# Tall Strassen sets: third sum formed in place, first sum asked for earlier, p5 ahead of q6, gate reads in program order

## The chip, the cores and the metric

The kernel runs on one core of one Trainium2 chip. A core has five engines that run their own instruction streams and meet at semaphores: PE (TensorE, matrix products), DVE (VectorE), ACT (ScalarE), POOL (GpSimd) and SP (SyncE), the last of which only issues DMA transfers here. The profile shows PE's weight loads apart as PEld. The metric is the device time of one execution in microseconds (us).

## The reference

One block of a hybrid network on 512 tokens of width 1024, all in float32. Cut to what matters here:

```python
x = x + 0.5 * swiglu(rmsnorm(x, g1), ffn1_w_gu, ffn1_w_down)
h = rmsnorm(x, g_mix)
z = h @ w_in                                  # 1024 x IN_COLS
cb, cc, cu, q, k, v, g_lr, r, ga, gb = split(z)
y_conv = (cb * causal_short_conv(cc * cu, conv_w)) @ w_out_conv
log_a = log_sigmoid(g_lr @ gate_w_up + gate_b) / 16
o = gla_chunked(q, k, v, log_a)               # 4 heads, chunks of 64 tokens
o = norm_per_head(o) * gla_norm_g
y_gla = (o * silu(r)) @ w_out_gla
merged = sigmoid(ga) * y_conv + sigmoid(gb) * y_gla
x = x + merged @ w_o
x = x + 0.5 * swiglu(rmsnorm(x, g2), ffn2_w_gu, ffn2_w_down)
return rmsnorm(x, g_final)
```

The change lies in the middle part: the products for v, ga, gb (columns of `w_in`, each 1024 x 1024) and `w_out_conv`, called out here.

## The kernel before

**Products.** Every float32 product is made of three matmuls on parts of the operands: a high part (a cast) and a low part (the operand less its high part). For a block of weights ACT makes the high part `wh` (L380) and DVE the low part `wl` (L381); three buffers of each are there. PE multiplies high x high, high x low and low x high.

**Sets of seven.** Most products are made in sets: the weights are cut in four blocks a11, a12, a21, a22 (512 KB each), and seven products of sums of blocks, m1 p2 q6 p5 q7 p3 p4, take the place of eight. A set needs these weight operands:

- m1: a11; then POOL asks for a transfer that accumulates in SBUF, a11 += a21 (`add`, L355; a21 holds a21 + a22 by then)
- p2: a12; then a12 += a11
- q6: a11 as it is by then; p5: a21, which is a21 + a22; p4: a22; p3: a12 as it is by then
- q7: s3 = a11 + a21 of the first values, made by DVE into a fifth tile (L365)

So a set has three accumulating transfers on POOL's queue: a21 += a22 (asked right after L365), a11 += a21 (after m1's low part), a12 += a11 (after p2's low part and a11's sum).

**Tall sets.** v, ga, gb and out are "tall": each has two halves, s = 0 and 1, with weights of their own, and their products alternate (`tall`): m1 of half 0, m1 of half 1, p2 of half 0, and so on, 14 steps of 12 matmuls of 128x512 on PE (L691). The other sets (conv, cb, r; PE line L575) have one half and 24 matmuls of 128x256 a step. In time the order is: v, ga, gb, then conv 0 to 3, cb, r, and out, and then the set for `w_out_gla`.

**What sets the order.** `Weights(2)` issues, while PE is at one step, the weight work of the step two places ahead: loads on SP's queue (L351) into tiles named f (ten in the pool), sums, cast and low part. Each engine takes its instructions in order, so a waiting instruction holds all behind it. A dictionary of hooks hangs pieces of the attention behind named steps: `gates`, `decays`, `scale`, `scores`, `state`, `output`, `squares` for each of four heads. `state` multiplies on PE (L1249) and copies from PSUM on DVE (L1252); `scale` and `decays` are chains on DVE (L546, L1190, L1193) and ACT. Results ga and gb are written to DRAM and read back by `gate()` on SP's queue (L1522), with a sigmoid on ACT behind it. A scheduler may move instructions against this order where data allow it; `keep_in_program_order` forbids it for one instruction.

**Loads of a tall set.** Half 0 is loaded four steps ahead of its m1 and half 1 three, and at m1 itself (issue step i) L365 and a21 += a22 are issued.

Of the kernel before, what the change touches and what calls it, by code (L numbers as in the profile page):

```python
# [12 lines left out]
ALU = mybir.AluOpType  # L13
# [56 lines left out]
def unit_cols(u):  # L70
    return u[2] * len(u[3]) * u[4]
# [57 lines left out]

TALL_ORDER = ("m1", "p2", "q6", "p5", "q7", "p3", "p4")
TALL = {}


# [81 lines left out]
def block_kernel(ctx: ExitStack, tc: tile.TileContext, xT, vecs, gf, gup, wgl, wts, out):  # L217
    nc = tc.nc
# [78 lines left out]
    class Weights:  # L297
# [3 lines left out]
        def __init__(self, ahead):  # L301
            self.ahead = ahead
            self.issued = 0
            self.taken = 0
            self.end = 0
            self.ready = []
            self.raw = {}
            self.loads = {}
            self.sums = {}
            self.pre = {}  # L310

        def phase(self, early, first=6):


            self.early = early
            lo, self.end = self.end, [e for e in ENDS if e > self.end][0]
            for i in range(lo, self.end):
                n, p = STEPS[i]
                if p == "m1" and i in CHUNK_STEP.values():
                    at = CHUNK_STEP[0, "m1"]  # L320
                    self.loads.setdefault(at - (4 if i == at else 2), []).append(n)
                    self.sums.setdefault(i, []).append(n)
                elif p == "m1" and n in TALL:
                    self.loads.setdefault(i - (4, 3)[TALL[n][1]], []).append(n)
                    self.sums.setdefault(i, []).append(n)
                elif p is None and i > lo and STEPS[i - 1][1] is not None and self.end < len(STEPS):
                    self.pre.setdefault(i - 4, []).append(n)
                elif p == "m1":
                    self.loads.setdefault(max(lo, i - first), []).append(n)
                    first = 6  # L330
                    self.sums.setdefault(max(lo + 3, i - 3), []).append(n)
            if self.end == len(STEPS):
                c = CHUNK_STEP
                for i, at in enumerate((c[1, "q6"], c[1, "p3"], c[1, "p3"], c[1, "p4"])):
                    self.pre.setdefault(at, []).append(STEPS[self.end - TAIL + i][0])
            self.fetch(lo)
# [20 lines left out]
        def issue(self):  # L357
            at = self.issued
            self.fetch(at)
            for n in self.loads.get(at, ()):  # L360
                self.raw[n] = [self.dma(n + i) for i in range(4)]
            for n in self.sums.get(at, ()):
                self.raw[n].append(tile_of("f", [P, 1024]))
                a11, a12, a21, a22, s3 = self.raw[n]
                nc.vector.tensor_tensor(out=s3, in0=a11, in1=a21, op=ALU.add)  # L365
                self.add(a21, a22)
            for n in self.pre.get(at, ()):
                self.raw[n] = self.dma(n)
            n, p = STEPS[at]
            w = unit_cols(PLAN[n])  # L370
            if p is None:
                raw = self.raw[n]
            else:
                a11, a12, a21, a22, s3 = (self.raw[n] + [None])[:5]
                raw = {"m1": a11, "p2": a12, "q6": a11, "p5": a21, "q7": s3, "p4": a22,
                       "p3": a12}[p]
            late = at >= len(STEPS) - TAIL
            h = tile_of("op" if late else "wh", [P, 1024], F32R)
            l = tile_of("op" if late else "wl", [P, 1024], F32R)
            nc.scalar.copy(h[:, :w], raw[:, :w])  # L380
            nc.vector.tensor_tensor(out=l[:, :w], in0=raw[:, :w], in1=h[:, :w].bitcast(F32),  # L381
                                    op=ALU.subtract)
            if p == "m1":
                self.add(a11, a21)
            if p == "p2":
                self.add(a12, a11)
            self.issued += 1
            self.ready.append((h, l))
# [657 lines left out]
    def mixer(norm, nxt):  # L1046
# [3 lines left out]
        gates_d = {n: dram.tile([KD, P, S], F32, tag=n, name=n) for n in ("ga", "gb")}  # L1050
# [19 lines left out]
        def G_tile(i, dtype=F32):  # L1070
# [13 lines left out]
            out=maskf, in_=maskf, pattern=[[1, P]], compare_op=ALU.is_ge, fill=0.0,  # L1084
# [13 lines left out]
        for i in range(2):  # L1098
# [3 lines left out]
                                    in1=gl_w[i][:, :, 0, :RANK].bitcast(F32), op=ALU.subtract)  # L1102
# [3 lines left out]
        for i in range(6):  # L1106
# [3 lines left out]
                                in1=gup_w[R2 : 2 * R2].bitcast(F32), op=ALU.subtract)  # L1110
# [18 lines left out]
        def evac_k(h, o):  # L1129
# [7 lines left out]
                                in1=glr[2 * R2 : R3].bitcast(F32), op=ALU.subtract)  # L1137
# [35 lines left out]
        def gates(h):  # L1173

            a = AUX()
            nc.tensor.matmul(a, gup_w[:R3, h * DK : (h + 1) * DK], glr[:R3],
                             start=True, stop=True)
            b = vec[:, V_GB + h : V_GB + h + 1]
            nc.scalar.activation(E, a, AF.Abs, bias=b)
            nc.vector.tensor_scalar(out=M, in0=a, scalar1=b, scalar2=0.0,  # L1180
                                    op0=ALU.add, op1=ALU.min)
            nc.scalar.activation(E, E, AF.Exp, scale=-1.0)
            nc.scalar.activation(E, E, AF.Ln, bias=1.0)
            nc.vector.tensor_tensor(out=M, in0=M, in1=E, op=ALU.subtract)
            nc.vector.tensor_tensor_scan(out=E, data0=reset, data1=M, initial=0.0,
                                         op0=ALU.mult, op1=ALU.add)
# [18 lines left out]
        def scale(h):  # L1205

            q_, k_ = QK[h][:, 0], QK[h][:, 1]
            ref, dc = sm4[:, 0], sm4[:, 1]  # L1210
            mul(q_, EX, q_)
            mul(KX, pairs(KS)[:, :, 0], pairs(k_)[:, :, 0])
            mul(QX, pairs(q_)[:, :, 1], bc(ref[:, :, 1]))
            mul(pairs(KS)[:, :, 1], pairs(KS)[:, :, 1], pairs(k_)[:, :, 1])
            mul(k_, M, k_)
            mul(pairs(KS)[:, :, 0], KX, bc(dc[:, :, 1]))
            mul(pairs(QS)[:, :, 1], QX, bc(dc[:, :, 0]))
            mul(pairs(QS)[:, :, 0], pairs(q_)[:, :, 0], bc(ref[:, :, 0]))
            mul(d2s, dc[:, :, 0], dc[:, :, 1])
# [59 lines left out]
        def squares(h):  # L1279

            sh, sl = split(E)
            st = AUX()
            nc.tensor.matmul(st, ones_r, sh, start=True, stop=False)
            nc.tensor.matmul(st, ones_r, sl, start=False, stop=True)
            nc.vector.transpose(E, st)
            nc.vector.tensor_scalar(
                out=vs[:, 16 * h : 16 * (h + 1)],
                in0=E.rearrange("p (b c) -> p b c", c=32)[:, :, 0],
                scalar1=1.0 / DV, scalar2=EPS, op0=ALU.mult, op1=ALU.add)
# [81 lines left out]
        def split_o(h):  # L1371
            for a, b in split_pair(O[h]):
                og_h.append(a)
                og_l.append(b)

        hooks = {
            ("v", 0, "q6"): [decays], ("v", 1, "p5"): [lambda: scale(0)],
            ("v", 1, "p3"): [lambda: scores(0)],
            ("ga", 1, "m1"): [lambda: state(0)], ("ga", 1, "p2"): [lambda: output(0)],
            ("ga", 0, "p5"): [lambda: squares(0)], ("ga", 0, "q7"): [lambda: gates(1)],  # L1380
            ("ga", 1, "q7"): [decays], ("ga", 1, "p3"): [lambda: scale(1)],
            ("gb", 0, "m1"): [lambda: scores(1)], ("gb", 0, "p2"): [lambda: state(1)],
            ("gb", 1, "q6"): [lambda: output(1)], ("gb", 1, "q7"): [lambda: squares(1)],
            ("gb", 0, "p3"): [move], ("gb", 0, "p4"): [lambda: gates(2)],
            ("gb", 1, "p4"): [decays], (0, "q6"): [lambda: scale(2)],
            (0, "p3"): [lambda: scores(2)], (1, "q6"): [lambda: state(2)],
            (1, "q7"): [lambda: output(2)], (1, "p3"): [lambda: squares(2)],
            (2, "q6"): [lambda: gates(3)], (2, "q7"): [decays], (2, "p3"): [lambda: scale(3)],
# [1 line left out]
            (4, "q6"): [lambda: output(3)], (4, "p3"): [lambda: squares(3)],  # L1390
            (5, "q7"): [lambda: normalise(0)], (5, "p3"): [lambda: normalise(1)],
            (6, "q7"): [lambda: normalise(2)], (6, "p3"): [lambda: normalise(3)],
            ("out", 1, "q6"): [lambda: co.make("p4")], ("out", 1, "p5"): [lambda: split_o(0)],
            ("out", 1, "q7"): [lambda: split_o(1)], ("out", 0, "p3"): [lambda: split_o(2)],
            ("out", 1, "p3"): [lambda: split_o(3)],
        }
# [117 lines left out]
        co = Operands(lambda j, l: YS[:, 4 * j : 4 * j + 4, 2 + l * HW : 2 + (l + 1) * HW])  # L1514
# [4 lines left out]

        def gate(name, t, e):  # L1520
            g = T()
            nc.sync.dma_start(g, gates_d[name][2 * t + e])  # L1522
            nc.scalar.activation(g, g, AF.Sigmoid)
            return g

# [31 lines left out]
        for e in range(2):  # L1557
            o = mm_wide("w_out_gla", KD, 512 * e, og_h, og_l, extra=between(e))
            for t in range(NTB):
                g = gate("gb", t, e)  # L1560
# [82 lines left out]
```

## Time and profile before

| | us |
|---|---|
| median of 3 runs | 1191.41 |
| lowest, highest | 1190.86, 1192.36 |
| the profiled execution | 1191.23 |
| its span in the trace | 1189.5 |

The profile is of one execution. Its page gives each engine's busy time; the view of waits says for how long PE stood idle and which instruction ended that; the timelines list instructions with start, duration and the idle time before them in brackets; the windows view gives the busy time of every engine in a stretch. Names such as `wl<-f,wh` are the program's own: output, then inputs, without buffer numbers. Lines L... are those of the kernel before.

The stages of interest, by PE: v from about 370 to 428 us, ga to 477, gb to 521, conv 0 from there, out from about 690 to 735.

### The profile page before, as it was taken

How to read it: one execution, taken by the hardware profiler on the slowest of the kernel's cores; microseconds unless marked ns; L12 is line 12 of the kernel's file. 1: busy time of each engine (PE TensorE's matmuls, PEld its weight loads, DVE VectorE, ACT ScalarE, POOL GpSimd, SP SyncE). 2: the span in 40 equal slices, each digit the busy share in tenths (PEclk: the TensorE clock that was granted, in tenths of full speed). 3: DMA queues.
4: the chain of work that ended last, by engine and by line, in shares of the span. 5: the costliest groups of instructions: out<-in, count | busy, mean ns of one | idle time of the engine just before them, and what ended most of it. 6: DMA issues, size and time to landing. Idle time of an engine off the chain costs nothing. (4 is left out here: it accounts for less than half of the span.)

```text
span 1189.5 us, 18127 instructions
## 1 busy us (share of the span) xinstructions
PE 1173.1 (99%) x7218; PEld 1052.5 (88%) x7218; DVE 917.9 (77%) x1132; ACT 619.3 (52%) x780; POOL 116.6 (10%) x155
## 2 busy tenths in 40 slices
PE   9999999999999999999999999999999999999997
PEld 8899999999988888789999997888889999998886
DVE  7987676989797976667787998556598767785686
ACT  6565455545452847464654568324356555572353
POOL 0011111011110110111010110100001111100100
PEclk9999999999999999999999999999999999999999
DMA  9378777656481885877567768712538777763431
GB/s 347 79 212 183 190 180 193 172 128 164 96 301 60 187 179 170 220 187 195 134 163 164 179 170 242 257 46 93 182 82 210 171 181 178 188 172 115 92 93 71
DMA packets 58148, 197.03 MB, mean 166 GB/s; under 512 B 6768, under 2 KB 6896, under 8 KB 58064
## 3 DMA queue, kind: packets, MB, share of 16 engines
q1 hardware_dynamic: 36912, 124.27, 31.0%
q0 software_dynamic: 18560, 67.12, 30.6%
q10 hardware_dynamic: 2592, 4.49, 1.0%
q8 instruction: 56, 0.92, 0.3%
q14 instruction: 28, 0.23, 0.1%
HBM read 124.55 MB, written 8.39 MB: 112 GB/s over the span
## 5 line engine op out<-in xcount | busy, mean ns | idle before, releaser
L380 ACT CAST wh<-f 128x1024 fp32r<-128x1024 f32 (+1 forms) x337 | 352.0, 1047 | 418.4 <-PE mm L575 93.2
L381 DVE TENSOR_TENSOR wl<-f,wh 128x1024 fp32r<-128x1024 f32 (+1 forms) x337 | 409.3, 1217 | 167.2 <-ACT wh L380 159.0
L575 PE MATMUL mm<-op,wh 128*128 128x256 f32 x1344 | 243.7, 284 | 0.8 <-ACT tp L580 0.8
L575 PEld LDWEIGHTS mm<-op,wh 128*128 128x128 f32 x1344 | 210.0, 192 | 1.5 <-ACT tp L580 1.0
L605 PE MATMUL mm<-op,wh 128*128 128x256 f32 x1152 | 209.7, 284 | 0.2 <-ACT tp L609 0.2
L355 POOL DMA_DIRECT2D f<-f x120 | 103.6, 869 | 947.4 <-DVE wl L381 457.7
L575 PE MATMUL mm<-op,wl 128*128 128x256 f32 x672 | 190.6, 284 | 1.4 <-DVE wl L381 1.4
L605 PEld LDWEIGHTS mm<-op,wh 128*128 128x128 f32 x1152 | 179.2, 191 | 2.1 <-ACT tp L609 0.6
L605 PE MATMUL mm<-op,wl 128*128 128x256 f32 x576 | 163.0, 283 | 0.1
L597 PE MATMUL mm<-op,wh 128*128 128x512 f32 x432 | 154.4, 398 | 0.0
L691 PE MATMUL mm<-wh,op 128*128 128x512 f32 x448 | 141.3, 391 | 0.8 <-ACT wh L380 0.8
L575 PEld LDWEIGHTS mm<-op,wl 128*128 128x128 f32 x672 | 128.9, 192 | 1.9 <-DVE wl L381 1.8
L599 PE MATMUL mm<-op,wl 128*128 128x256 f32 x432 | 121.4, 281 | 0.0
L605 PEld LDWEIGHTS mm<-op,wl 128*128 128x128 f32 x576 | 110.2, 191 | 0.3 <-DVE wl L381 0.3
L691 PEld LDWEIGHTS mm<-wh,op 128*128 128x128 f32 x448 | 84.1, 188 | 18.6 <-ACT wh L380 1.4
L597 PEld LDWEIGHTS mm<-op,wh 128*128 128x128 f32 x432 | 81.3, 188 | 18.2
L691 PE MATMUL mm<-wl,op 128*128 128x512 f32 x224 | 88.1, 393 | 1.7 <-DVE wl L381 1.7
L599 PEld LDWEIGHTS mm<-op,wl 128*128 128x128 f32 x432 | 81.7, 189 | 0.0
L432 PE MATMUL mm<-op,wh 128*128 128x512 f32 x256 | 64.3, 392 | 0.0
L408 PE MATMUL mm<-op,wh 128*128 128x512 f32 x164 | 63.8, 389 | 0.0
L409 PE MATMUL mm<-op,wh 128*128 128x512 f32 x164 | 63.8, 389 | 0.0
L410 PE MATMUL mm<-op,wl 128*128 128x512 f32 x164 | 63.8, 389 | 0.0
(288 smaller groups left out, 1641.8 us busy)
## 6 DMA issues: line engine op xcount, KB each, us to landing
f<-wts SPq DMA_DIRECT2D x219, 512.0 KB, 4.4
f<-f POOLq DMA_DIRECT2D x120, 512.0 KB, 5.0
X<-xT SPq DMA_DIRECT2D x8, 256.0 KB, 5.5
xs<-X POOLq DMA_DIRECT2D x8, 256.0 KB, 4.5
ga<-tp ACTq DMA_DIRECT2D x8, 256.0 KB, 2.4
gb<-tp ACTq DMA_DIRECT2D x8, 256.0 KB, 5.2
tp<-ga SPq DMA_DIRECT2D x8, 256.0 KB, 3.4
tp<-gb SPq DMA_DIRECT2D x8, 256.0 KB, 3.9
```

The lines of the kernel that those rows point to most:

```text
L355: nc.gpsimd.dma_start(out_, a, accum_op=ALU.add)
L380: nc.scalar.copy(h[:, :w], raw[:, :w])
L381: nc.vector.tensor_tensor(out=l[:, :w], in0=raw[:, :w], in1=h[:, :w].bitcast(F32), op=ALU.subtract)
L408: nc.tensor.matmul(o, wh, ah, start=first, stop=False)
L409: nc.tensor.matmul(o, wh, al, start=False, stop=False)
L410: nc.tensor.matmul(o, wl, ah, start=False, stop=last)
L432: nc.tensor.matmul(o[c], w[:, s : s + P], a[k], start=k == 0 and j == 0, stop=k == kt - 1 and j == 2)
L575: nc.tensor.matmul(to, ww[:, s], aa[:, t], start=fresh and k == 0 and e == 0 and j == 0, stop=k == 3 and j == 2, skip_group_check=True)
L597: nc.tensor.matmul(o[:, e], h[:, s], a, start=fresh and k == 0, stop=False, skip_group_check=True)
L599: nc.tensor.matmul(o[:, e, HW:], l[:, s], a[:, :HW], start=False, stop=k == 3, skip_group_check=True)
L605: nc.tensor.matmul(to, ww[:, s], aa, start=fresh and k == 0 and e == 0 and j == 0, stop=k == 3 and j == 2, skip_group_check=True)
L691: nc.tensor.matmul(self.bank[b][e], aa[:, c], ww, start=fresh and i == 0 and n == 0, stop=k == 3 and n == 2, skip_group_check=True)
```

## The change

1. In tall sets the fifth tile and L365 are gone. q7's operand is made in place from the sum in a11: a11 = (a11 + a21 + a22) − a22, by a DVE subtraction (line 381 of the new file), issued when q7's cast is. It follows the last readers of that sum: q6's cast and low part, and the transfer a12 += a11.
2. The first sum, a21 += a22, is asked for one issue step ahead of m1 in half 0 and in m1's own step in half 1 (two and three steps behind the loads), without waiting for a DVE instruction.
3. The order of the seven products in tall sets becomes m1 p2 p5 q6 q7 p3 p4.
4. Hooks of the fourth to seventh step are renamed to the products that now stand there; three move besides: gates(2) from behind (gb, 0, p4) to behind (gb, 1, p3), its `decays` from (gb, 1, p4) to (gb, 0, p4), and split_o(0) from (out, 1, p5) to (out, 0, q7).
5. The gate reads are kept in program order.

```diff
-TALL_ORDER = ("m1", "p2", "q6", "p5", "q7", "p3", "p4")
+TALL_ORDER = ("m1", "p2", "p5", "q6", "q7", "p3", "p4")
...
                 elif p == "m1" and n in TALL:
                     self.loads.setdefault(i - (4, 3)[TALL[n][1]], []).append(n)
-                    self.sums.setdefault(i, []).append(n)
+                    self.firsts.setdefault(i - (1, 0)[TALL[n][1]], []).append(n)
...
+            for n in self.firsts.get(at, ()):
+                self.add(self.raw[n][2], self.raw[n][3])
...
                 a11, a12, a21, a22, s3 = (self.raw[n] + [None])[:5]
+                if n in TALL:
+                    s3 = a11
+                    if p == "q7":
+                        nc.vector.tensor_tensor(out=a11, in0=a11, in1=a22, op=ALU.subtract)
...
-            ("v", 0, "q6"): [decays], ("v", 1, "p5"): [lambda: scale(0)],
+            ("v", 0, "p5"): [decays], ("v", 1, "q6"): [lambda: scale(0)],
...
-            ("ga", 0, "p5"): [lambda: squares(0)], ("ga", 0, "q7"): [lambda: gates(1)],
+            ("ga", 0, "q6"): [lambda: squares(0)], ("ga", 0, "q7"): [lambda: gates(1)],
...
-            ("gb", 1, "q6"): [lambda: output(1)], ("gb", 1, "q7"): [lambda: squares(1)],
-            ("gb", 0, "p3"): [move], ("gb", 0, "p4"): [lambda: gates(2)],
-            ("gb", 1, "p4"): [decays], (0, "q6"): [lambda: scale(2)],
+            ("gb", 1, "p5"): [lambda: output(1)], ("gb", 1, "q7"): [lambda: squares(1)],
+            ("gb", 0, "p3"): [move], ("gb", 1, "p3"): [lambda: gates(2)],
+            ("gb", 0, "p4"): [decays], (0, "q6"): [lambda: scale(2)],
...
-            ("out", 1, "q6"): [lambda: co.make("p4")], ("out", 1, "p5"): [lambda: split_o(0)],
+            ("out", 1, "q6"): [lambda: co.make("p4")], ("out", 0, "q7"): [lambda: split_o(0)],
...
             g = T()
-            nc.sync.dma_start(g, gates_d[name][2 * t + e])
+            tc.keep_in_program_order(nc.sync.dma_start(g, gates_d[name][2 * t + e]))
```

What this does to the order on the engines is shown at three places. The new file's lines are seven higher than those of before from L381 on (L352 is the load, L388 the low part, L553 the pieces of `decays` and `scale`, L698 the tall matmuls, L1234 and L1235 the scores, L1529 the gate reads).

**The start of gb.** On DVE before, from the last piece of `scale` for the second head: f671 and f680 are a11 of the two halves, f673 and f682 a21, and wl690, wl693 the low parts of m1.

```order
L546 TENSOR_TENSOR d2_3905<-sm_3904 128x4
L365 TENSOR_TENSOR f688_4695<-f671_4585,f673_4589 128x1024
L381 TENSOR_TENSOR wl690_4699<-f671_4585,wh689_4698 128x1024
L365 TENSOR_TENSOR f691_4715<-f680_4642,f682_4646 128x1024
L381 TENSOR_TENSOR wl693_4719<-f680_4642,wh692_4718 128x1024
```

The same place of the change, where f667 and f676 are a11 of the two halves:

```order
L553 TENSOR_TENSOR d2_3905<-sm_3904 128x4
L388 TENSOR_TENSOR wl685_4693<-f667_4581,wh684_4692 128x1024
L388 TENSOR_TENSOR wl687_4711<-f676_4638,wh686_4710 128x1024
L388 TENSOR_TENSOR wl693_4736<-f668_4583,wh692_4735 128x1024
L388 TENSOR_TENSOR wl697_4768<-f677_4640,wh696_4767 128x1024
```

On PE before, at the same place, the first two matmuls of m1 and then the scores hook:

```order
L691 MATMUL mm637_4396<-wh686_4666,op619_4293 128x512
L691 MATMUL mm696_4741<-wh689_4698,op564_3949 128x512
L691 MATMUL mm697_4742<-wh689_4698,op564_3949 128x512
L1227 MATMUL aux700_4760<-y508_3669 128x128
L1228 MATMUL aux700_4760<-g3_555_3902 64x64
```

On PE in the change, the first five matmuls of m1; seven more follow, and then the scores hook:

```order
L698 MATMUL mm633_4390<-wh682_4663,op617_4291 128x512
L698 MATMUL mm690_4733<-wh684_4692,op564_3949 128x512
L698 MATMUL mm690_4733<-wl685_4693,op564_3949 128x512
L698 MATMUL mm690_4733<-wh684_4692,op565_3950 128x512
L698 MATMUL mm691_4734<-wh684_4692,op564_3949 128x512
L698 MATMUL mm691_4734<-wl685_4693,op564_3949 128x512
```

The two L365 are gone from DVE, the low parts stand directly behind the backlog of `scale`, and on PE the matmul that reads the low part of m1 stands second, where before the whole hook lay ahead of it.

**q6 and q7 in gb.** On DVE in the change: wl711 and wl717 are the low parts of q6 in the two halves, L381 the subtractions in place, wl723 the low part of q7 in half 0.

```order
L388 TENSOR_TENSOR wl711_4837<-f667_4581,wh710_4836 128x1024
L381 TENSOR_TENSOR f667_4581<-f667_4581,f670_4587 128x1024
L388 TENSOR_TENSOR wl717_4861<-f676_4638,wh716_4860 128x1024
L381 TENSOR_TENSOR f676_4638<-f676_4638,f679_4644 128x1024
L388 TENSOR_TENSOR wl723_4905<-f667_4581,wh722_4904 128x1024
```

The subtraction of one half and the low part of q7 in that half have the other half's work between them.

**The gate reads.** On SP before, at the loads of out (f991 to f994) and the reads of ga and gb:

```order
L351 DMA f993_6977<-wts 128x1024
L351 DMA f994_6979<-wts 128x1024
L1522 DMA tp1079_7466<-ga_3659 128x512
L1522 DMA tp1083_7500<-ga_3659 128x512
L1522 DMA tp1087_7522<-ga_3659 128x512
L1522 DMA tp1091_7556<-ga_3659 128x512
L1522 DMA tp1092_7572<-gb_3660 128x512
L1522 DMA tp1093_7577<-gb_3660 128x512
L351 DMA f1049_7299<-wts 128x1024
```

On SP in the change, where f987 and f988 are the last loads of out:

```order
L352 DMA f987_6971<-wts 128x1024
L352 DMA f988_6973<-wts 128x1024
L352 DMA f1039_7287<-wts 128x1024
L352 DMA f1056_7373<-wts 128x1024
L352 DMA f1057_7375<-wts 128x1024
L352 DMA f1058_7377<-wts 128x1024
L352 DMA f1061_7395<-wts 128x1024
L352 DMA f1068_7419<-wts 128x1024
L1529 DMA tp1071_7458<-ga_3659 128x512
L352 DMA f1072_7462<-wts 128x1024
L1529 DMA tp1075_7492<-ga_3659 128x512
```

Six reads that stood ahead of the first weights for `w_out_gla` (f1049 before, f1039 in the change) now stand behind six of these loads.

More of the change, by code (lines that the diff above doesn't have):

```diff
@@ L310, in __init__ @@
             self.pre = {}
+            self.firsts = {}
         def phase(self, early, first=6):
```

## The prediction

> **What bounds the kernel now.** I read the page's first part, then PE's waits, then the timelines of PE, DVE, ACT, POOL and SP around the waits that lie in the tall sets. The page:
> ```profile
> span 1189.5 us, 18127 instructions
> PE 1173.1 (99%) x7218; PEld 1052.5 (88%) x7218; DVE 917.9 (77%) x1132; ACT 619.3 (52%) x780; POOL 116.6 (10%) x155
> ```
> PE is busy almost throughout, and the change takes no matmul away. Only PE's idle time can be won, and this is all of it that has a releaser (us in total, times, longest):
> ```profile
> PE aux L1249 <- DVE g L1252: 2.9, 1, 2.9
> PE mm L691 <- DVE wl L381: 1.7, 2, 1.0
> PE mm L575 <- DVE wl L381: 1.4, 2, 0.8
> PE aux L282 <- POOL ones L279: 1.1, 1, 1.1
> PE mm L575 <- ACT tp L580: 0.8, 1, 0.8
> PE mm L691 <- ACT wh L380: 0.8, 1, 0.8
> PE aux L1227 <- DVE qk L546: 0.5, 1, 0.5
> ```
> The sum is 9.2 us, 0.8% of the span: with some tenths of restart at each wait, no version of this change can win much more than that. L282 is the start of the kernel; the wait on L580, the one on qk and 0.6 of the 1.4 us on L575 lie in the conv, cb and r sets, whose instructions stand in the same order as before. They stay.
>
> Call the accumulating transfers S1 (a21 += a22), S2 (a11 += a21) and S3 (a12 += a11). The largest wait, in gb (DVE, ACT, POOL, PE rows; start, duration, and in brackets the idle time before):
> ```profile
> 477.94 1.22 DVE L365 TENSOR_TENSOR f<-f,f 128x1024 f32<-128x1024 f32 x1
> 479.07 1.22 DVE L381 TENSOR_TENSOR wl<-f,wh 128x1024 fp32r<-128x1024 f32 x1
> 480.21 1.22 DVE L365 TENSOR_TENSOR f<-f,f 128x1024 f32<-128x1024 f32 x1
> 490.80 1.23 DVE L381 TENSOR_TENSOR wl<-f,wh 128x1024 fp32r<-128x1024 f32 x1 [5.36 <-ACT wh L380]
> 491.94 0.42 DVE L1252 COPY g<-aux 128x256 f32<-128x256 f32 x1
> 489.73 1.04 ACT L380 CAST wh<-f 128x1024 fp32r<-128x1024 f32 x1 [3.42 <-DMA f<-f]
> 479.45 0.86 POOL L355 DMA_DIRECT2D f<-f  x1 [28.03 <-DVE f L365]
> 481.95 0.86 POOL L355 DMA_DIRECT2D f<-f  x1 [1.64 <-DVE f L365]
> 484.54 0.86 POOL L355 DMA_DIRECT2D f<-f  x1 [1.72 <-ACT wh L380]
> 487.30 0.86 POOL L355 DMA_DIRECT2D f<-f  x1 [1.90 <-issue]
> 488.90 0.58 PE L691 MATMUL mm<-wh,op 128*128 128x512 f32 x1
> 492.42 0.70 PE L1249 MATMUL aux<-y,g 128*128 128x256 f32 x2 [2.93 <-DVE g L1252]
> ```
> Read backwards: PE waits for the copy L1252, which stands on DVE behind the low part of q6; that waits for q6's cast, and the cast for S2, asked at 484.54 and landed at 489.73 (5.2 us). S2 is late because S1 stood behind L365, which DVE reached only at 477.94. The copy itself needed none of this: it is held only by its place in a queue.
>
> **The change, part by part.**
>
> *A, the wait in gb.* Without L365, S1 waits for its loads alone. POOL had sat idle 28 us before 479.45, so S1 moves before m1's turn. S2 then waits for m1's low part, the last reader of a11 ahead of it: it ends near 478.7 (below), so S2 is asked about 480 and lands about 485 by the 5.2 us above. It is also wanted later: with p5 ahead of q6, two steps of 12 matmuls lie between. Three matmuls take 0.68 us (next fence, 476.81 to 477.49), so two steps are 5.4 us, and q6's cast is due near 492. Even an S2 as late as before (489.73) would fit. From 488.90 to 492.42 PE started one matmul in 3.52 us; less about 0.4 for a usual hand-over, **3.1 us go**. Bounds: 0 if another wait falls on the copy, 3.3.
>
> *The new wait in gb m1.* This is what comes in its place.
> ```profile
> 465.00:478.00 13.00, 13.00 (x60) 10.70 (x58) 12.29 (x22) 10.78 (x16) 0.00 (x0) 1.00 0.42 154
> 476.81 0.84 PE L691 MATMUL mm<-wh,op 128*128 128x512 f32 x3
> 477.49 0.38 PE L1227 MATMUL aux<-y 128*128 128x128 f32 x2
> 480.39 0.48 PE L691 MATMUL mm<-wl,op 128*128 128x512 f32 x1
> ```
> In the windows view (PE, PEld, DVE, ACT, POOL busy) DVE was busy 12.29 of 13 us before 478: a backlog of the second head's decay and scale pieces and the low parts. Before, PE started two matmuls of gb m1, which need only the cast, then ran the scores hook from 477.49 to 480.39, and the low part (479.07 + 1.22 = 480.29) came just in time. Now the order has all twelve matmuls of m1 ahead of that hook, and the second of them needs the low part, at about 477.3. Without L365 ahead of it the low part would run from 477.94 to 479.16 if nothing else moved; the hook gates(1), one place earlier in ga, lets the chain start a little sooner (about 0.45 us, my estimate from DVE's idle 0.71 in those 13 us). So it ends near 478.7 and PE waits **1.4 us**. Bounds: 1.9 if nothing moves; 0 if the backlog comes a whole step (2.7 us) earlier. I take the value near the upper end, since a queue that is 95% busy cannot move up by a step.
>
> *B, conv0 q7.*
> ```profile
> 527.71 0.68 ACT L1179 ACTIVATE g<-aux,vec 128x512 f32<-128x512 f32 x1
> 538.18 1.22 DVE L381 TENSOR_TENSOR wl<-f,wh 128x1024 fp32r<-128x1024 f32 x1
> 539.45 0.38 PE L575 MATMUL mm<-op,wl 128*128 128x256 f32 x1 [0.81 <-DVE wl L381]
> ```
> The third head's gates start on ACT at 527.71 and their decays and scale hold DVE until 538.18, when q7's low part begins; PE waits 0.81. Gates(2) and its decays now stand a step earlier, 2.7 us at least. That exceeds the wait, so 0.81 and the restart (0.2, see C) go: **1.0 us**. What is late next is conv0 p2's low part, with about half a microsecond in hand by the same count. Bounds: 0 and 1.1.
>
> *C, the out set.*
> ```profile
> 702.08 0.86 POOL L355 DMA_DIRECT2D f<-f  x1 [5.84 <-DVE f L365]
> 707.50 1.75 POOL L355 DMA_DIRECT2D f<-f  x2 [4.57 <-DMA tp<-ga]
> 716.85 1.75 POOL L355 DMA_DIRECT2D f<-f  x2 [7.60 <-issue]
> 704.65 5.53 SPq L1522 DMA_DIRECT2D tp<-ga  x4
> 710.46 2.42 SPq L1522 DMA_DIRECT2D tp<-gb  x2
> 724.15 0.33 SPq L351 DMA_DIRECT2D f<-wts  x1
> 721.52 1.05 ACT L380 CAST wh<-f 128x1024 fp32r<-128x1024 f32 x1 [4.60 <-DMA f<-f]
> 722.62 0.50 PE L691 MATMUL mm<-wh,op 128*128 128x512 f32 x1 [0.76 <-ACT wh L380]
> 723.88 0.50 PE L691 MATMUL mm<-wl,op 128*128 128x512 f32 x1 [0.76 <-DVE wl L381]
> 731.74 0.65 PE L691 MATMUL mm<-wh,op 128*128 128x512 f32 x2
> 733.35 0.50 PE L691 MATMUL mm<-wl,op 128*128 128x512 f32 x1 [0.96 <-DVE wl L381]
> ```
> S1 of the second half was asked second in the pair at 707.50, behind an L365, and S2 could follow only at 716.85: some 8.4 us for S1, beside six gate reads (704.65 to 712.9), against 5.2 in gb. S2 landed at 721.52, and PE waited for cast and low part, and again for q7's. One matmul took 1.26 us from 722.62 to 723.88, and two 1.61 from 731.74 to 733.35, where the pace is 0.23: 1.03 and 1.15 lost; the first wait is 0.76 plus the same restart, 0.9 to 1.0. Together **3.1 us go**. In the changed order S1 is asked with no L365 ahead, both S2 by about 707 and landed by 711 to 716, and q6's casts are due near 719 and 722. Bounds: 0 and 3.3. S1 to S3 and the casts need only f tiles; the six gate reads now stand behind six weight loads. With eight tiles of out instead of ten in a pool of ten, two of these loads can start early (none did before 724.15): 1 MB, where the six reads of 256 KB were 1.5 MB.
>
> The Trainium skill, "DMA: Bandwidth & Descriptors", section "Issuing engines are not separate DMA queues", says that transfers of SP and POOL run on the same 16 engines and interleave, so a place behind other loads on SP reserves nothing for POOL's sums. By that rule S1 and S2 could again take 8.4 us instead of 5.2. The trace agrees so far, in the 8.4 us above. The sum would not be lost even so, since q6 s1 is due 5.4 us later.
>
> *In-place subtraction.* Eight L365 of 1.22 us go and eight subtractions of the same shape come: DVE's load is the same, and I price them as L365's 1.22. What differs is the place: the subtraction must follow q6's low part and the landing of S3, and q7's cast follows it. In v there is least cover:
> ```profile
> 370.00:428.00 58.00, 58.00 (x263) 47.50 (x262) 56.46 (x68) 34.70 (x42) 6.03 (x7) 1.00 0.57 134
> ```
> DVE is busy 56.46 of 58 us there and PE does not wait. The order sets the other half's low part between a subtraction and the low part that needs it, so a cast (1.05) lies beside 1.22 of DVE work. I take 0 for v, and 0.2 for the ends of ga and for q7 in out, where my count of DVE's queue leaves less than 0.5 us. Bounds: 0, and 1.05 for each of eight (8.4), the rival below.
>
> *Gate reads and the sigmoid* on ACT stand ahead of casts; a read that came late would hold these. By the order they are asked while the out set still runs, and the products that use them follow by several steps: 0. That cover gone, the price is the reading's lateness once, up to the 5.53 us that four took above.
>
> **The sum:** 3.1 + 1.0 + 3.1 − 1.4 − 0.2 = 5.6 us less than the profiled execution's 1191.23 (span 1189.5 and 1.7 around it): 1185.6. That execution lies 0.2 under the median of 1191.41, so I predict **1185.8 us**.
>
> **The rivals.**
> - *All goes and nothing comes:* DVE's backlog before gb m1 clears earlier. Gain 7.2 us, 1184.2. Against it: the 12.29 of 13 us.
> - *Half is given back:* C stays because weight loads take the gate reads' part beside the sums, or ga and out wait on DVE for about 3 us more. Gain 5.6 − 3.1 = 2.5 to 4 us, about 1188. For it: DVE is near full in v and at the end of ga; against it the 5.4 us of delay that q6 gets.
> - *The waits only move:* the scores hook was what hid DVE's backlog in gb, so the wait at m1 takes A whole, and in out the subtraction takes the place of L365 in the same queue (C stays). Gain about 1.0, to 2: 1190. For it: both places had DVE late before any transfer was.
> - *Slower, the lock-step of q7:* subtraction, cast, low part follow one another, 1.22 + 1.05 + 1.22 = 3.5 us against a step of 2.7. If DVE finds nothing to do beside the cast, each of eight steps loses about 1.05, 8.4 us, and with m1's 1.4 this exceeds the 7.2 won: 7.2 − 1.4 − 8.4 is 2.6 us slower, 1194. It decides once the loss for each passes 0.7 us (5.6 / 8), where no gain is left; past 1.0 (8.0 / 8) it shows. Against it: the interleaving of the two halves. That the change does nothing of what it says is excluded by the order; the third rival is nearest to it.
>
> **How the numbers follow.** Forecast (gain 4.5 to 6.7) 0.48; all goes 0.12; half given back 0.18; waits only move 0.15; slower 0.07. A measurement of this kernel tells about 0.2%, 2.4 us, from no change, so faster means under 1189.0: 0.48 + 0.12 + 0.18 = 0.78; within 0.15; slower 0.07. The range, 1183.5 to 1189.5, holds the first three and a little of the fourth, some 8 in 10.
>
> **What would show it.** Right: no wait of L1249 on L1252; POOL's S1 in gb well before 475; no brackets on L691 around the out set's q6 and q7; the exponentials of gates(2) on ACT at least 2.7 us nearer to the end of gb; and a new bracket of 1 to 2 us <- DVE wl at the first low-part matmul of gb m1. Wrong: a bracket on q7 in v or ga, DVE idle before the new subtraction "<- DMA f<-f", or casts that wait for a gate read. Most doubtful are the 1.4 and the 3.1 of C, which rest on my walk through the queues' order.

## The result, and the profile after

| | us |
|---|---|
| before, median of 5 runs | 1192.12 |
| the change, median of 5 runs | 1186.1 (lowest 1185.51) |
| ratio, 95% interval | 0.995 (0.9934 to 0.9965) |
| the profiled execution shown below, its span | 1185.41, 1183.7 |

The change makes the kernel 6.0 us faster, 0.5%; 1185.8 was predicted. Between the two profiled executions, 1191.23 and 1185.41, it is 5.8 us. One execution of the change took 1929.49 us at a granted clock of 0.556 (without it the median of the other four is 1185.92), and the profile of the change shown here is that of the run e0_change, the same kernel at a clock of 0.998.

The page of the change, its first lines:

```profile
span 1183.7 us, 18120 instructions
PE 1172.6 (99%) x7218; PEld 1051.9 (89%) x7218; DVE 919.3 (78%) x1132; ACT 620.7 (52%) x780; POOL 116.7 (10%) x155
```

And all of its waits of PE that have a releaser (us in total, times, longest us):

```profile
PE aux L282 <- POOL ones L279: 1.1, 1, 1.1
PE mm L698 <- DVE wl L388: 1.0, 1, 1.0
PE mm L582 <- ACT tp L587: 0.8, 1, 0.8
PE mm L582 <- DVE wl L388: 0.6, 1, 0.6
PE aux L1234 <- DVE qk L553: 0.5, 1, 0.5
```

The engines' work is the same. The list is what has changed: the 2.9 us on the state hook's copy, 0.8 of the 1.4 on L575 (now L582), and the waits of the out set are gone. (The list of before has one more row than the prediction shows, 0.2 us on L605 far ahead of these sets; it is absent here too.) One is new, 1.0 us on a low part in a tall set. It stands where gb begins. The timelines of the change there, PE and then DVE, and POOL's sums of gb, with the state hook on PE at the end:

```profile
476.76 0.61 PE L698 MATMUL mm<-wh,op 128*128 128x512 f32 x2
478.37 0.50 PE L698 MATMUL mm<-wl,op 128*128 128x512 f32 x1 [0.99 <-DVE wl L388]
477.03 0.15 DVE L553 TENSOR_TENSOR d<-sm 128x4 f32<-128x4 f32 x1
477.10 1.21 DVE L388 TENSOR_TENSOR wl<-f,wh 128x1024 fp32r<-128x1024 f32 x1
...
450.21 0.86 POOL L356 DMA_DIRECT2D f<-f  x1 [3.19 <-DMA f<-wts]
472.71 0.86 POOL L356 DMA_DIRECT2D f<-f  x1 [21.52 <-DVE g L553]
478.61 0.86 POOL L356 DMA_DIRECT2D f<-f  x1 [5.04 <-DVE wl L388]
480.97 0.86 POOL L356 DMA_DIRECT2D f<-f  x1 [1.50 <-DVE wl L388]
...
490.58 0.70 PE L1256 MATMUL aux<-y,g 128*128 128x256 f32 x2
```

The low part of m1 starts when the last piece of scale is through and ends at 478.31; PE wanted it at about 477.2. From the matmul that started at 476.99 (the second of the pair at 476.76) to the next at 478.37 are 1.38 us where 0.23 is the pace: 1.15 lost. The first sums are asked at 450.21 and 472.71, before m1's turn, and a11 += a21 at 478.61 and 480.97. The state hook at 490.58 has no bracket any more. On PE the out set lasted 41.5 us before, from its first matmul at 708.07 to the first of the next set at 749.60, and lasts 38.4 now, from 705.36 to 743.78.

### The profile page after: what moved, and what is told of

Read it like the earlier page. It is cut to its first block, busy times and chain, and to the rows that moved or that the text cites. A ratio compares the mean times of both kernels' runs of the same rounds, so it can differ in the third digit from the quotient of the medians.

```text
span 1927.8 us, 18120 instructions
## 1 busy us (share of the span) xinstructions
PE 1919.6 (100%) x7218; PEld 1456.4 (76%) x7218; DVE 938.7 (49%) x1132; ACT 623.2 (32%) x780; POOL 115.5 (6%) x155
## 4 chain that ended last, share of the span: by engine, by line
PE 99%; DMA 0%; ACT 0%; DVE 0%; issue 0%
PE mm L582 20%; PE mm L612 17%; PE mm L698 13%; PE mm L604 9%; PE mm L439 8%; PE mm L606 4%; PE mm L984 3%; PE mm L415 3%; PE mm L417 3%; PE mm L416 3%; PE mm L934 2%; PE mm L933 2%; PE mm L935 2%; PE mm L457 1%; PE mm L456 1%; PE mm L458 1%
## 5 line engine op out<-in xcount | busy, mean ns | idle before, releaser
L388 DVE TENSOR_TENSOR wl<-f,wh 128x1024 fp32r<-128x1024 f32 (+1 forms) x337 | 410.9, 1220 | 528.0 <-ACT wh L387 499.1
L582 PE MATMUL mm<-op,wh 128*128 128x256 f32 x1344 | 375.7, 384 | 0.0
L582 PEld LDWEIGHTS mm<-op,wh 128*128 128x128 f32 x1344 | 324.3, 289 | 2.5 <-issue 1.0
L612 PE MATMUL mm<-op,wh 128*128 128x256 f32 x1152 | 322.0, 384 | 0.0
L612 PEld LDWEIGHTS mm<-op,wh 128*128 128x128 f32 x1152 | 271.5, 279 | 6.4 <-issue 3.0
L582 PE MATMUL mm<-op,wl 128*128 128x256 f32 x672 | 257.9, 384 | 0.0
L604 PE MATMUL mm<-op,wh 128*128 128x512 f32 x432 | 240.4, 574 | 0.0
L612 PE MATMUL mm<-op,wl 128*128 128x256 f32 x576 | 220.7, 383 | 0.0
L698 PE MATMUL mm<-wh,op 128*128 128x512 f32 x448 | 219.3, 579 | 0.0
L582 PEld LDWEIGHTS mm<-op,wl 128*128 128x128 f32 x672 | 195.2, 290 | 0.4 <-issue 0.2
L606 PE MATMUL mm<-op,wl 128*128 128x256 f32 x432 | 166.3, 385 | 0.0
L612 PEld LDWEIGHTS mm<-op,wl 128*128 128x128 f32 x576 | 162.3, 282 | 0.3
L698 PEld LDWEIGHTS mm<-wh,op 128*128 128x128 f32 x448 | 98.1, 219 | 73.2 <-issue 42.0
L604 PEld LDWEIGHTS mm<-op,wh 128*128 128x128 f32 x432 | 97.4, 225 | 59.3 <-issue 26.8
L698 PE MATMUL mm<-wl,op 128*128 128x512 f32 x224 | 129.7, 579 | 0.0
L439 PE MATMUL mm<-op,wh 128*128 128x512 f32 x256 | 104.8, 576 | 0.2 <-DVE op L490 0.2
L606 PEld LDWEIGHTS mm<-op,wl 128*128 128x128 f32 x432 | 99.5, 230 | 2.6
L415 PE MATMUL mm<-op,wh 128*128 128x512 f32 x164 | 94.6, 577 | 0.0
L416 PE MATMUL mm<-op,wh 128*128 128x512 f32 x164 | 94.3, 575 | 0.0
L417 PE MATMUL mm<-op,wl 128*128 128x512 f32 x164 | 94.3, 575 | 0.0
```

The lines of the kernel that those rows point to most:

```text
L415: nc.tensor.matmul(o, wh, ah, start=first, stop=False)
L416: nc.tensor.matmul(o, wh, al, start=False, stop=False)
L417: nc.tensor.matmul(o, wl, ah, start=False, stop=last)
L439: nc.tensor.matmul(o[c], w[:, s : s + P], a[k], start=k == 0 and j == 0, stop=k == kt - 1 and j == 2)
L582: nc.tensor.matmul(to, ww[:, s], aa[:, t], start=fresh and k == 0 and e == 0 and j == 0, stop=k == 3 and j == 2, skip_group_check=True)
L604: nc.tensor.matmul(o[:, e], h[:, s], a, start=fresh and k == 0, stop=False, skip_group_check=True)
```

## Experiments

The runs are called e0 to e11, in the order in which they stand here. Each lists the median of its executions; the kernel before had medians of 1192.39, 1192.40, 1191.95 and 1191.35 us beside the four groups of runs, in the order below, and the change 1185.68.

### The change again, for its profile

> The changed kernel itself, for a profile at the full clock. My forecast: no wait of the state hook's matmul in gb (was 2.9 us), none of conv0 q7 (0.8), none in the out set's q6 and q7 (2.5); a new wait of 1.4 us (0 to 1.9) on the low part of gb m1; span 1183.9 to 1184.5. Rival 'all goes and nothing comes': no wait at gb m1, and some other new loss of about 1 us elsewhere that explains the same time, for example restarts or waits at the ends of v, ga and out.

Measured 1185.68 us (ratio 0.9944, 0.9926 to 0.9962), the profile above. The forecast waits went, the new one came and is 1.0 us of idle time, 1.15 with the restart, for the 1.4 that was expected. At 471.61, 507.83 and 727.32 a matmul started about 0.2 us late without any wait in the list: the 0.2 us of other losses was some 0.5.

### The third sum by L365, as before

> The change with the third sum made as before, by L365 at m1's step into a fifth tile, with a21 += a22 behind it; the new order p5 q6, the hooks and the gate reads stay. Theory 'the order alone is enough': a11 += a21 lands as late as before (near 490 in gb, 721 in out) but q6 is due 5.4 us later, so the waits in gb and out stay away; time within 1.5 us of the change (1185 to 1188). Rival 'the early first sum did it': the waits of 2.9 us in gb and 2.5 in out come back at least by half; time 1189 or more.

```diff
-                    self.firsts.setdefault(i - (1, 0)[TALL[n][1]], []).append(n)
+                    self.sums.setdefault(i, []).append(n)
...
-                if n in TALL:
-                    s3 = a11
-                    if p == "q7":
-                        nc.vector.tensor_tensor(out=a11, in0=a11, in1=a22, op=ALU.subtract)
```

Measured 1187.72 us (0.9956, 0.9941 to 0.9972). No wait at the state hook, though the sums are as late as before (POOL's first sum of gb at 478.64, once L365 is through, a11 += a21 at 483.72): the order alone removes the largest wait. Most of the 2 us by which this version is slower are lost at the end of out and the start of the set behind it (ACT, then PE):

```profile
734.92 0.63 ACT L1526 ACTIVATE tp<-tp 128x512 f32<-128x512 f32 x1 [2.58 <-DMA tp<-ga]
735.46 1.03 ACT L383 CAST wh<-f 128x1024 fp32r<-128x1024 f32 x1
738.71 0.63 ACT L1526 ACTIVATE tp<-tp 128x512 f32<-128x512 f32 x1 [2.21 <-DMA tp<-ga]
739.24 1.04 ACT L383 CAST wh<-f 128x1024 fp32r<-128x1024 f32 x1
...
741.59 0.50 PE L694 MATMUL mm<-wl,op 128*128 128x512 f32 x1 [0.54 <-DVE wl L384]
...
744.73 0.51 PE L452 MATMUL mm<-wh,op 128*128 128x512 f32 x1 [0.34 <-ACT wh L383]
745.99 0.50 PE L453 MATMUL mm<-wl,op 128*128 128x512 f32 x1 [0.75 <-DVE wl L384]
```

A gate read lands late, its sigmoid holds ACT up by 2 us and more, and the cast of the next weights stands behind the sigmoid. This is the price that the prediction named for gate reads whose cover is gone. The reads were late because the loads ahead of them on SP were, and one of these waited for a sum. SP's waits from 720.8 to 728 us show it:

```profile
SPq L352 <- DMA f<-f: 7.0, 1, 7.0
```

The sum is a12 += a11 of the second half: it was asked at 716.67 and landed 11.2 us later, where it took 6.7 in the change. The load at 727.95 followed its landing, and two more loads and the first gate read stood behind that load, the read at 729.33.

### The old order of products

> The change with the products of tall sets in the old order m1 p2 q6 p5 (hooks at the same steps as before); in-place third sum, early first sum, gates(2) and gate reads as in the change. Theory 'the early first sum alone is enough': a11 += a21 lands near 485 in gb and before 716 in out, ahead of q6's cast at its old place; no wait in gb's state hook or in out's q6; time within 1.5 us of the change. Rival 'the order did it': the waits come back at least by half (3 us or more); time 1189 or more.

```diff
-TALL_ORDER = ("m1", "p2", "p5", "q6", "q7", "p3", "p4")
+TALL_ORDER = ("m1", "p2", "q6", "p5", "q7", "p3", "p4")
```

(with the hooks renamed accordingly). Measured 1186.15 us (0.9947, 0.9929 to 0.9966); 0.4 us of wait remain at the state hook, 0.7 at gb m1, none in out, and 0.6 come at the set behind out. So in gb the early sum by itself does nearly as much as the order by itself; the two parts of the change cover the same wait twice. (Run e5 below has neither and keeps the 2.9 us.)

### Gate reads left to the scheduler

> The change with the gate reads left to the scheduler, which puts six of them ahead of the first weights for w_out_gla again. Forecast (their place is worth nothing, q6 has 5.4 us more): within 0.6 us of the change, no wait in out's q6 and q7. Rival 'the gate reads beside the sums were the wait in out': the 2.5 us of waits in out come back, 1188.5 or more.

```diff
-            tc.keep_in_program_order(nc.sync.dma_start(g, gates_d[name][2 * t + e]))
+            nc.sync.dma_start(g, gates_d[name][2 * t + e])
```

Measured 1188.54 us (0.9965, 0.9952 to 0.9978): 2.9 us slower than the change. The forecast fell. SP, POOL, DVE, ACT and PE rows of this run, in out:

```profile
702.38 3.85 SPq L1529 DMA_DIRECT2D tp<-ga  x4
707.02 3.19 SPq L1529 DMA_DIRECT2D tp<-gb  x2
...
718.47 0.86 POOL L356 DMA_DIRECT2D f<-f  x1 [3.32 <-DVE qk L1317]
...
726.59 1.23 DVE L381 TENSOR_TENSOR f<-f,f 128x1024 f32<-128x1024 f32 x1 [1.97 <-issue]
727.92 1.04 ACT L387 CAST wh<-f 128x1024 fp32r<-128x1024 f32 x1 [1.22 <-DVE f L381]
728.88 1.08 ACT L1315 ACTIVATE qk<-mm 128x512 f32<-128x512 f32 x2
...
729.52 0.49 PE L698 MATMUL mm<-wh,op 128*128 128x512 f32 x1 [1.79 <-ACT qk L1315]
```

Read downwards this is one chain. The last sum, a12 += a11 of the second half, is asked at 718.47 (in the change at 714.04) and lands at 726.51. The subtraction in place has to wait for it and starts at 726.59; in the change the sum had landed at 720.72, 2.3 us ahead of the same subtraction. The cast of q7 waits for the subtraction, a copy of finished products out of PSUM stands behind the cast on ACT, and PE waits for the copy. The old waits, at q6 and at the low part of q7, do not come back: this one is new.

The sum was late because the one ahead of it was. In both runs a12 += a11 is asked 0.5 us after a11 += a21 of its half has landed. That one was asked at 709.54 here and at 708.63 in the change, and took, in this run and then in the change:

```profile
DMA to landing us min/median/max: 8.4/8.4/8.4
```

```profile
DMA to landing us min/median/max: 4.9/4.9/4.9
```

Here the six gate reads, asked from 702.38 to 709.89, stood beside it. So it landed 4.4 us later. The last sum itself took 8.0 us, 1.4 more than in the change, though the six reads had landed by 718.14; why is not shown. The two views of DMA from 698 to 728 us, of the change and of this run (count, size, median us to landing), show all five sums and what stood beside them:

```profile
f<-f POOLq DMA_DIRECT2D x5, 512.0 KB, 6.7
```

```profile
f<-f POOLq DMA_DIRECT2D x5, 512.0 KB, 8.0
tp<-ga SPq DMA_DIRECT2D x4, 256.0 KB, 8.9
tp<-gb SPq DMA_DIRECT2D x2, 256.0 KB, 8.2
```

### gates(2) and its decays at their old steps

> The change with gates(2) and its decays back behind (gb, 0, p4) and (gb, 1, p4). Forecast: conv0's q7 waits for its low part again, 0.8 us of PE idle, 1.0 with the restart; everything else as in the change; span about 1184.7. Rival 'the third head's gates came early anyway, since gb itself is shorter': no wait there, same time as the change.

```diff
-            ("gb", 0, "p3"): [move], ("gb", 1, "p3"): [lambda: gates(2)],
-            ("gb", 0, "p4"): [decays], (0, "q6"): [lambda: scale(2)],
+            ("gb", 0, "p3"): [move], ("gb", 0, "p4"): [lambda: gates(2)],
+            ("gb", 1, "p4"): [decays], (0, "q6"): [lambda: scale(2)],
```

Measured 1187.22 us (0.9959, 0.9944 to 0.9974), 1.5 more than the change. The row of conv0 q7 is back as forecast, and with the same size as in the kernel before:

```profile
537.88 0.39 PE L582 MATMUL mm<-op,wl 128*128 128x256 f32 x1 [0.81 <-DVE wl L388]
```

Of the other 0.5 us its list of waits has 0.3 at the set behind out and 0.7 in the first feed-forward part, which the edit does not touch; they are not explained here.

### The kernel before, with only the gate reads in order

> The kernel before with only the gate reads kept in program order, behind the first weights for w_out_gla. If the late L365 alone makes the wait in out, the 2.5 us of waits there stay, and with ten tiles full the reads come later than 724: same time or slower. If the six gate reads beside the sum made it (8.4 us for a21 += a22 of the second half), that sum takes about 5 us, a11 += a21 lands near 718, and the waits at q6 go: about 2 us faster, 1190. Either way late gate reads may hold casts of the next set, as in the run that kept L365.

The edit is the reverse of that in e3, made in the kernel before. Measured 1191.64 us, 0.9993 (0.9984 to 1.0003): no difference that can be told. But the profile is not the same. Its waits in tall sets and at the set behind out:

```profile
PE aux L1249 <- DVE g L1252: 2.9, 1, 2.9
PE mm L449 <- ACT wh L380: 0.8, 1, 0.8
PE mm L450 <- DVE wl L381: 0.8, 1, 0.8
```

All three waits of out are gone, by this part alone and with L365 in place: a21 += a22 of the second half is asked at 709.95 and lands 6.1 us later, where it took 7.9 (the prediction's 8.4 was the time until the next sum was asked). What was won is given back at once, two waits of 0.8 us, since gate reads now come late to the set behind out: a sigmoid there waits 3.96 us for its read, with a cast behind it.

### scale(1) and scores(1) one step later

> The change with scale(1) one step later (behind ga p4 of half 0) and scores(1) one step later (behind gb m1 of half 1). On DVE the low part of gb m1 of half 0 then stands ahead of the chain of scale. Theory 'DVE's backlog makes the wait at gb m1': the wait of 1.0 us there goes and none comes at m1 of half 1 or at the scores hook; span 1182.6, time 1184.5. Rival 'the queue is simply full': the wait moves to m1 of half 1, to the scores or to the state hook, and the time stays within 0.3 us.

```diff
-            ("ga", 1, "q7"): [decays], ("ga", 1, "p3"): [lambda: scale(1)],
-            ("gb", 0, "m1"): [lambda: scores(1)], ("gb", 0, "p2"): [lambda: state(1)],
+            ("ga", 1, "q7"): [decays], ("ga", 0, "p4"): [lambda: scale(1)],
+            ("gb", 1, "m1"): [lambda: scores(1)], ("gb", 0, "p2"): [lambda: state(1)],
```

Measured 1185.05 us (1184.45 to 1185.44; ratio 0.9939, 0.9925 to 0.9953). DVE's rows:

```profile
475.27 1.21 DVE L388 TENSOR_TENSOR wl<-f,wh 128x1024 fp32r<-128x1024 f32 x1
476.40 0.41 DVE L553 TENSOR_TENSOR g<-g,y 128x256 f32<-128x256 f32 x1
...
478.68 0.15 DVE L553 TENSOR_TENSOR d<-sm 128x4 f32<-128x4 f32 x1
478.75 2.35 DVE L388 TENSOR_TENSOR wl<-f,wh 128x1024 fp32r<-128x1024 f32 x2
```

The low part of m1 (475.27) stands ahead of the rest of the chain, and PE has no wait at gb m1, at m1 of the other half, or at the hooks. It was the order of DVE's queue, not its load. The median is 0.6 us under the change's, half of the 1.2 that were forecast. The profiled span is 1183.5, not 1182.6: that execution was the slowest of five, and lost 0.4 us at the set behind out.

### A fifth tile in out again

> The change, but in the out set the third sum a11 - a22 goes into a fifth tile that is taken at m1, so ten of ten f tiles are held there and the subtraction need not wait for a12 += a11. Gate reads stay behind the weight loads. Theory 'the two spare tiles are what lets the gate reads stand behind weight loads': the loads and with them the gate reads come later, sigmoids hold the casts at the start of the next set, and 1.5 to 2.7 us of waits come at 740 to 750, as in the run that kept L365; time 1187.2 to 1188.5. Rival 'the loss there came from L365 and its late sum': no wait there, time as the change.

```diff
+                if n in TALL and TALL[n][0] == "out" and p == "m1":
+                    self.raw[n].append(tile_of("f", [P, 1024]))
                 a11, a12, a21, a22, s3 = (self.raw[n] + [None])[:5]
-                if n in TALL:
+                if n in TALL and TALL[n][0] != "out":
                     s3 = a11
-                    if p == "q7":
-                        nc.vector.tensor_tensor(out=a11, in0=a11, in1=a22, op=ALU.subtract)
+                if n in TALL and p == "q7":
+                    nc.vector.tensor_tensor(out=s3, in0=a11, in1=a22, op=ALU.subtract)
```

Measured 1185.66 us (0.9947, 0.9934 to 0.9961): as the change, with no wait at the set behind out. My theory fell. The two spare tiles are not what lets the gate reads stand behind weight loads. It fits with what SP waited for in e1: here a12 += a11 of the second half lands at 717.08, where it landed at 727.89 there, and the first gate read is asked at 727.74. That the late sum makes the loss in e1 is read from the traces; no run changes that sum alone.

### scores(3) later as well

> The version with scale(1) and scores(1) a step later, and scores(3) one place later too (behind p5 of conv 3 in place of q6). If the wait of 0.5 us on qk at the scores of the fourth head is only a place in PE's order, it goes (0.6 with the restart): span about 0.6 us under that version's, time 1184.4. Rival: the state hook behind it or the low parts of conv 3 wait instead, same time.

```diff
-            (3, "q6"): [lambda: scores(3)], (3, "p3"): [lambda: state(3)],
+            (3, "p5"): [lambda: scores(3)], (3, "p3"): [lambda: state(3)],
```

Measured 1184.62 us (0.9936, 0.9922 to 0.9949), the lowest median of all, though its interval overlaps that of e6. The 0.5 us on qk are no longer among its waits; 0.6 us stand at the set behind out, where e6 has 0.2.

### The fifth tile in out, and gate reads free

> As the run with the fifth tile in out, but with the gate reads left to the scheduler, so six of them stand ahead of the weights again. Against the run with free gate reads alone (1188.5, waits of 1.8 and 0.4 us at q7 of half 1) the subtraction here does not read or write what a12 += a11 still uses. Theory 'in that run the late a12 += a11 held the subtraction, and this the casts behind it on ACT': the 1.8 and 0.4 go, no gate read is late at the next set, time 1186 or less. Rival 'the gate reads delay every sum, whichever reads it': waits of 2 us or more stay in out, on q6 or p3, time 1188 or more.

Measured 1192.16 us (1.0004, 0.9995 to 1.0013). The time and the waits are the rival's: against e7, from which only the reads' place differs, 6.5 us are lost, nearly all of it in out.

```profile
PE mm L700 <- ACT qk L1317: 2.8, 1, 2.8
PE mm L700 <- DVE wl L390: 2.4, 3, 1.0
```

(1.0 of the 2.4 us is the wait at gb m1, which e7 has too.) The sums are slowed as the rival says: a11 += a21 of the two halves took 5.2 and 5.3 us to landing in e7 and 8.2 and 8.9 here. But the wait of 2.8 us is not theirs alone. The copy for which PE waits (731.56) stands on ACT behind a sigmoid (731.02) that sat 1.03 us for a gate read asked only at 725.92. As a test of who reads the late sum the run is spoiled, since the subtraction also moved up DVE's queue, where it waited 1.53 and 1.49 us for a11 += a21 ahead of low parts.

### Sigmoids, not reads, in program order

> The change with the sigmoids kept in program order on ACT instead of the gate reads on SP. The order then puts six reads behind two weight loads and ahead of four, near 717 to 722, after the sums were asked; the sigmoids stand on ACT where the change has them. Theory 'the reads cost by standing beside the sums at 702 to 710 and by the sigmoids that come with them ahead of copies and casts': neither is so here, no wait in out, and the reads are no longer late at the next set (ACT idle on them was 12.5 us from 725 to 760): time as the change, 1185.7, or up to 0.3 less. Rival 'any read ahead of the weights costs': waits of 2 us or more in out or on the late weights at the next set, 1187.7 or more.

```diff
-            tc.keep_in_program_order(nc.sync.dma_start(g, gates_d[name][2 * t + e]))
-            nc.scalar.activation(g, g, AF.Sigmoid)
+            nc.sync.dma_start(g, gates_d[name][2 * t + e])
+            tc.keep_in_program_order(nc.scalar.activation(g, g, AF.Sigmoid))
```

I had the time of the reads wrong: the two loads ahead of them went out early, one at 701.50, and the reads followed at 702.11 to 709.9, as in e3. That made it a cleaner test than planned, for no sigmoid stands on ACT in out here. Measured 1187.62 us (0.9966, 0.9952 to 0.9979). DVE's timeline in out, and the wait of PE that follows:

```profile
726.26 1.23 DVE L381 TENSOR_TENSOR f<-f,f 128x1024 f32<-128x1024 f32 x1 [2.99 <-issue]
```

```profile
PE mm L698 <- ACT qk L1315: 1.8, 1, 1.8
```

The same wait of 1.8 us as in e3, with the subtraction waiting for a12 += a11 (asked at 718.19). So the sigmoids are not needed for it; the reads beside the sums are enough. The 0.4 us that e3 lost at the set behind out are absent here, where the reads are early and the sigmoids late.

> The version with scale(1), scores(1) and scores(3) later, and the sigmoids instead of the gate reads in program order. If the run beside it shows no cost, this loses the wait of 0.6 us at the start of the next set (741 to 743) that its parent has: time 1184.0. Otherwise 1186 or more.

Its edits are those of e8 and e10 together. Measured 1185.83 us (0.9946, 0.9931 to 0.9962): 1.2 us behind e8, with the same wait (1.6 us) in out.

## Why the prediction was right, and where not

The time was right, 1185.8 for 1186.1, and so were most of its terms:

- **A, 3.1 us:** right. The wait of 2.9 us is gone, a11 += a21 was asked at 478.61 and 480.97 where about 480 was said. That even a late sum would fit behind p5 was shown by e1. Four runs show that either part is enough: 2.9 us of wait with neither (e5), none with the order alone (e1), 0.4 with the early sum alone (e2), none with both.
- **The new wait at gb m1, 1.4 us:** right in place and cause (e6), a little large: 1.15. The chain on DVE ended at 477.1 and not at 477.5.
- **B, 1.0 us:** right; gates(2) begins on ACT at 520.54 where it was 527.71, and e4 brings back the 0.81 exactly.
- **In-place subtraction:** nothing in v, as said; no lock-step at q7 anywhere in the change. The mechanism that the rival feared, a subtraction that holds the cast, appeared in e3 and e10, by way of a late sum.
- **Gate reads, 0:** right on PE in the change, though one sign that was named for "wrong" did show, casts behind a sigmoid that waits for its read: ACT idles 12.5 us in all for gate reads between 725 and 760 us, and no wait of PE comes of it. Where the reads come later, in e1 and e5, it does.
- **C, 3.1 us:** the size was right, 41.5 to 38.4 us for out on PE. The reason was right by half, and what it missed is the step that failed. The earlier sums and the later q6 do clear the old waits, since e3, without part 5, has none of them; but part 5 alone clears them too (e5). And without part 5 the change makes a wait of its own, the 1.8 us of e3 at q7, and 2.9 us of the whole gain are lost. I priced the reads' move at 0 and q7 in out at a part of 0.2; that the 3.1 came out even so is luck, since part 5 happened to be in the change. The sentence "The sum would not be lost even so, since q6 s1 is due 5.4 us later" holds for a11 += a21 and its reader q6: in e3 that sum took 8.4 us and q6 did not wait. But the next sum, a12 += a11, is asked behind it and got a new reader in the same change, the subtraction in place at q7. In the change it lands 2.3 us ahead of that reader and not 5.4; in e3 it was asked 4.4 us later.

Reads asked on SP slowed sums asked on POOL: a11 += a21 of the second half took 8.4 us to landing in e3 and 8.5 in e10 instead of 4.9, and 8.9 in e9 instead of 5.3 in e7. This agrees with the rule of the Trainium skill that was weighed there ("DMA: Bandwidth & Descriptors", section "Issuing engines are not separate DMA queues"). Where I set its consequence aside, the runs did not.

One more thing differs in out that neither the list of moved hooks nor C has: `co.make("p4")` kept its label, ("out", 1, "q6"), and so moved from the third product to the fourth. In e2 it is at the third again, and no wait in out comes back.

Of the other rivals, "all goes" fails at gb m1 and "the waits only move" holds in one place only, gb m1, for 1.15 of the 3.1 us. Of "half is given back" nothing came: two weight loads did go out beside the last sum of out (715.15 and 716.28), and PE did not wait there.

## What to carry to other kernels

When an operand is made in place, list its new readers and writers and give each transfer that they wait for its own slack; slack of one reader of a chain of sums says nothing of the next, and a sum that is late hands its lateness on. A change of several parts may cover one wait twice (early sum and later product) and bring a new one that only a part that looks incidental keeps away (the place of some reads in a queue): undo the parts one by one before saying which did it. A wait behind an engine's backlog is often mended by the order of two instructions in its queue rather than by less work.

## What was not expected

The first sum of gb's second half was asked only at 472.71, not well before 475 as that of the first half, at 450.21. The bracket there names a piece of scale on DVE, but the last load that the sum needs had gone out on SP only at 468.05, when a low part on DVE was through (466.82 and 1.20 us), and landed 4.1 us later. The sum followed by about 0.6 us, as other sums follow the landing they wait for by 0.5.

And in the kernel before, keeping the reads behind the loads cured three waits in out and caused two behind it, 0.8 us each, for no change in time. Why the same place costs nothing in the change is answered in part. There the first gate read is asked at 728.12 and lands 11.0 us ahead of the first matmul of the set behind out (743.78). In e5 and e1 it lands 9.5 and 9.8 us ahead, since SP had waited for late sums before it, 23.2 us in a row in e5 and 7.0 in e1. Why two of the later versions wait 0.6 us at that set, e2 and e8, stays open.
